# S5 stage: float32 products on two column tiles, and the order of the last gate

## The chip, the cores and the metric

One core of one Trainium2 chip runs the whole kernel. The metric is device time in microseconds, the median of the runs shown. An execution is also profiled: the profile gives its span, from the first instruction to the last, and each engine's work within it. The engines are PE (matrix products, with PEld for the loading of its stationary operand), DVE (vector), ACT (activations), POOL and SP (which only issues DMAs here).

## The reference, cut to what matters

Two layers on 256 tokens of width 1024, batch 1. Each layer adds half a SwiGLU block, a mixer, and half a SwiGLU block again to `h`. The mixer of the first layer is S5, a diagonal state-space layer, and the change lies in it; the second layer's mixer is attention.

```python
def s5_mixer(h, w_in, ..., w_glu, w_out):
    u = h @ w_in                                   # 64 groups of 16 channels
    ...                                            # lam, bb: discretised state matrices
    bu = einsum('bcgn,gpn->bcgp', u_c, bb)         # complex, 64 states a group
    st = associative_scan(lam * previous + bu)     # over the 256 positions
    y = einsum('bcgp,gnp->bcgn', st_re, c_re) - einsum('bcgp,gnp->bcgn', st_im, c_im)
    y = y + d_skip * u
    g = gelu(y)
    g = g * sigmoid(g @ w_glu)
    return g @ w_out
```

## The kernel before, in words

**Order of work.** The kernel is written as one program whose order on each engine is the order of the Python calls; nothing reorders it. Four positions are taken as one step of the scan, so 256 tokens are 64 steps, and every S5 product moves 64 columns. The 64 groups are worked in eight blocks `b` of four pairs of groups (`q`). The tables (`TA`, `TE`, `TB`) are made in the first SwiGLU stage, kept in DRAM and loaded by SP.

**Weights.** The large matrix products use two float32r parts of each float32 weight, a high part (`whi`) and a low part (`wlo`), and of each activation likewise. `Stream` brings the weights: SP loads a raw unit of 128 x 2048 into one of three buffers, and `split` cuts half a unit into `whi` (ACT, L84, or L90 where a gain is applied) and `wlo` (DVE, L85, or L91). `pump` does the next split in order if a slot is free, `get` fetches the two parts, `release` gives the slot back, and the second split of a unit frees the raw buffer for SP's next load. Where the calls of `pump` stand decides where the splits stand in the queues of ACT and DVE.

**The S5 stage.** In this order on PE, with the others beside it:

- `w_in(nh, t)`: four products of `h` with `w_in` into `psM`; ACT and DVE bring the result into `U`, 32 rows of channels a block.
- `t1(b)` (L982): eight float32 products, `TA` stationary (128 x 128) and `U` moving (64 columns), into an accumulator bank.
- `rot(b)`: DVE multiplies by `TE` (L1002 and L1003 from PSUM, L1004 and L1005 in SBUF) and scans (L1007, twice); POOL multiplies back in four instructions (L1011 to L1014) and leaves the states `hr`.
- `y_out(b)` (L1039 to L1041): for each of four `q` three float32 products, of `TB` with `U` and with the two parts of `hr`, into one `psR`; ACT applies the gelu (L1045, `yg`), DVE transposes (L1048, `gs`).
- `g_tr(b)`: two PE transposes (L1057) into a `psR`; ACT takes the high part (L1059, `xa`), DVE the low part (L1060), then ACT a float32 copy (L1061, `gf`). `psR` has two buffers in turn; at this place `y_out` has one of them and `g_tr` the other.
- `glu(b)` (L1074 to L1076): block `b` of `g @ w_glu`, 24 products of 256 columns, three for each of eight output chunks `o`, into four accumulator banks (two chunks a bank).
- `gate(i)`: for bank `i`, ACT's sigmoid (L1087), then DVE multiplies (L1089), makes the high part (L1091) and the low part (L1092).
- `so(b, t, n)`: the product with `w_out`, stationary from gate `b`'s output, 12 products of 512 columns for `b` of four and every `t` and half; the last two `b` run inside `boundary`, which adds the result to `h` (L369) and prepares the next stage's `x` by transposes (`prep`, L331, L333, L334).

From block 3 on one turn of the loop is

```python
for b in range(3, NB):
    y_out(b)
    glu(b - 3)
    if b + 3 < NB:
        t1rot(b + 3)
    g_tr(b - 1)
```

After it come `glu(5)`, `g_tr(7)`, a small activation that loads the sigmoid table (`warm`, L232), `glu(6)` and `glu(7)`, with `gate(i)` after each second chunk of `glu(7)`, then `so`. The dictionary `XO` gives, for each stage, the column at which the high and low parts of its `x` begin in their tile; `'g'` is that of the S5 gate.

Of the kernel before, what the change touches and what calls it, by code (L numbers as in the profile page):

```python
# [12 lines left out]
AF = mybir.ActivationFunctionType  # L13
# [12 lines left out]
TWO_PI = 2.0 * math.pi  # L26
MAGIC = 12582912.0

XO = {'f00': 124, 's5': 124, 'g': 0, 'f01': 80, 'f10': 8, 'moba': 124, 'f11': 8}
AO = (68, 68, 68, 68)  # L30
OO = 68

# [86 lines left out]
def trunk_kernel(ctx: ExitStack, tc, x, ffn_norm, ffn_w_gate, ffn_w_up, ffn_w_down, mix_norm,  # L119
# [17 lines left out]
    def psR():  # L137
        return pp.tile([128, 512], F32, name="pR", tag="R", bufs=2)
# [4 lines left out]
    mm = nc.tensor.matmul  # L143
# [85 lines left out]
    def warm(func):  # L229

        w = sp.tile([128, 1], F32, name="warm", tag="warm", bufs=1)
        nc.scalar.activation(w, ones[:, 0:1], func)  # L232
# [44 lines left out]
    st = Stream(nc, units, rp, hp)  # L277
# [37 lines left out]
    def home(pool, ph):  # L315

        xa = pool.tile([128, 4224], F32R, name="xa")
        v = xa[:, XO[ph]:XO[ph] + 4096].rearrange("p (i k c) -> p i k c", i=2, c=256)
        return v[:, 0], v[:, 1]

    def prep(t, n, ph, sq=True):

        if (ph, "x") not in X:
            X.clear()
            X[ph, "x"] = True
            X["h"], X["l"] = home(XP[0], ph)
        hh = h[t][:, n * 512:(n + 1) * 512]
        ps = psR()
        pv = ps.rearrange("p (k c) -> p k c", c=128)
        for k in range(4):  # L330
            nc.tensor.transpose(pv[:, k, :], hh[:, k * 128:(k + 1) * 128], ident)  # L331
        xh, xl = (X[p][:, n * 4:n * 4 + 4, t * 128:t * 128 + 128] for p in "hl")
        nc.scalar.activation(xh, pv, AF.Copy)  # L333
        nc.vector.tensor_tensor(xl, pv, xh.bitcast(F32), op=OP.subtract)  # L334
        if sq:
            squares(t, n)

    def squares(t, n):
        if n == 0:
            SS[t] = sp.tile([128, 2], F32, name="ss", tag="ss", bufs=4)  # L340
        hh = h[t][:, n * 512:(n + 1) * 512]
        sq = sp.tile([128, 512], mybir.dt.bfloat16, name="sq", tag="sq", bufs=1)
        nc.scalar.activation(sq, hh, AF.Square, accum_out=SS[t][:, n:n + 1])  # L343
        if n == 1:
            v = sp.tile([128, 1], F32, name="ms", tag="ms", bufs=4)
            nc.gpsimd.tensor_tensor(v, SS[t][:, 0:1], SS[t][:, 1:2], op=OP.add)  # L346
            nc.gpsimd.tensor_scalar(v, v, 1.0 / D, EPS, op0=OP.mult, op1=OP.add)
            r = sp.tile([128, 1], F32, name="rr", tag="rr", bufs=4)
            rsq(r, v, 1)
            Rr[t] = r  # L350
# [17 lines left out]
        hh = h[t][:, n * 512:(n + 1) * 512]  # L368
        nc.vector.scalar_tensor_tensor(hh, acc, scale, hh, op0=OP.mult, op1=OP.add)  # L369

    def boundary(nxt, parts, acc, scale, mid=None):

        if nxt is not None and nxt[0] == "f":
            order = [(0, 0), (1, 0), (0, 1), (1, 1)]
        else:
            order = [(0, 0), (0, 1), (1, 0), (1, 1)]
        for i in range(2):
            for part in parts[:-1]:
                part(*order[i])
            if mid is not None and i == 0:  # L380
                mid()
        for i, (t, n) in enumerate(order):
            for part in parts[-1:] if i < 2 else parts:
                part(t, n)
            finish(t, n, acc[2 * t + n], scale)
            if nxt is None:
                store(t, n)
            elif i:
                prep(*order[i - 1], nxt)

    def entry_hooks(ph):
        return {2: [lambda: prep(1, 1, ph)]}
# [562 lines left out]

    def s5(nxt, entry):
        V, P = nc.vector, nc.gpsimd
        wstack = ExitStack()
        wp = wstack.enter_context(tc.tile_pool(name="s5", bufs=1))
        S, H = {}, {}  # L960
        GT, GS = {}, {}
        acc = [None] * 4

        U = wp.tile([128, 32, 2, 32], F32, name="U")
# [11 lines left out]
        def t1(b):  # L976
            tv = TA.pop(b).rearrange("p (i q c) -> p i q c", i=2, c=128)
            ps = psA(b) if b < 4 else psM()
            for i in range(2):
                for q in range(4):  # L980
                    c = i * 256 + q * 64
                    mm(ps[:, c:c + 64], tv[:, i, q, :], U[:, 4 * b + q, :, :], start=True, stop=True)  # L982
            S[b] = ps

        def rot(b):
# [45 lines left out]
        def y_out(b):  # L1031
            tb = TB.pop(b)
            v2 = tb[:, 0:1024].rearrange("p (i q c) -> p i q c", i=2, c=128)
            v3 = tb[:, 1024:1536].rearrange("p (q c) -> p q c", c=128)
            ps = psR()
            hr = H.pop(b)
            for q in range(4):
                o = ps[:, q * 64:(q + 1) * 64]
                mm(o, v3[:, q, :], U[:, 4 * b + q, :, :], start=True, stop=False)  # L1039
                mm(o, v2[:, 0, q, :], hr[:, 0, q, :], start=False, stop=False)  # L1040
                mm(o, v2[:, 1, q, :], hr[:, 1, q, :], start=False, stop=True)  # L1041
            if b + 3 < NB:
                ld_b(b + 3)
            yg = wp.tile([128, 4, 2, 32], F32, name="yg", bufs=1)
            nc.scalar.activation(yg.rearrange("p q t c -> p (q t c)"), ps[:, 0:256], AF.Gelu_apprx_tanh)  # L1045
            gs = wp.tile([128, 2, 4, 32], F32, name="gs", bufs=2)
            for t in range(2):
                V.transpose(gs[:, t], yg[:, :, t, :])  # L1048
            GS[b] = gs

        def g_tr(b):
            ps = psR()
            gs = GS.pop(b)
            if b == 0:
                GT["h"], GT["l"] = home(xp, "g")
            for t in range(2):
                nc.tensor.transpose(ps[:, t * 128:(t + 1) * 128], gs[:, t].rearrange("p q c -> p (q c)"),  # L1057
                                    ident)
            nc.scalar.activation(GT["h"][:, b, :], ps[:, 0:256], AF.Copy)  # L1059
            V.tensor_tensor(GT["l"][:, b, :], ps[:, 0:256], GT["h"][:, b, :].bitcast(F32), op=OP.subtract)  # L1060
            nc.scalar.activation(gf[b // 2][:, b % 2, :], ps[:, 0:256], AF.Copy)  # L1061

        def glu(b, after=None):

            u = where["glu", b // 2]
            if b == 0:
                for i in range(4):
                    acc[i] = psA(i)
            gh, gl = GT["h"][:, b, :], GT["l"][:, b, :]
            wh, wl = st.get(u, b % 2)  # L1070
            for o in range(8):
                d = acc[o // 2][:, (o % 2) * 256:(o % 2) * 256 + 256]
                c = slice(o * 128, o * 128 + 128)
                mm(d, wh[:, c], gh, start=b == 0 and o % 2 == 0, stop=False, skip_group_check=True)  # L1074
                mm(d, wh[:, c], gl, start=False, stop=False, skip_group_check=True)
                mm(d, wl[:, c], gh, start=False, stop=b == NB - 1, skip_group_check=True)  # L1076
                if o == 7:
                    st.release(u, b % 2)
                if o == 3 and b < 7 or o == 7 and b in (3, 4, 5):
                    st.pump()  # L1080
                if after is not None and o % 2 == 1:
                    after(o // 2)

        def gate(i):

            sg = fp.tile([128, 2, 256], F32, name="sg", tag="gr", bufs=2)
            nc.scalar.activation(sg, acc[i].rearrange("p (a c) -> p a c", a=2), AF.Sigmoid)  # L1087
            g = gf[i]
            V.tensor_tensor(g, g, sg, op=OP.mult)  # L1089
            gh, gl = (GT[p][:, 2 * i:2 * i + 2, :] for p in "hl")  # L1090
            V.tensor_copy(gh, g)  # L1091
            V.tensor_tensor(gl, g, gh.bitcast(F32), op=OP.subtract)  # L1092

        def so(b, t, n, last=False):
            u = where["so", b]
            if b == 0:
                acc[2 * t + n] = psA(2 * t + n)
            gh, gl = (GT[p][:, 2 * b:2 * b + 2, :] for p in "hl")
            bank_mm(acc, t, n, gh, gl, u, [0, 1], b == 0, last)
# [20 lines left out]
        wstack.close()  # L1120
        lstack.close()
        XP[0] = xstack.enter_context(tc.tile_pool(name="xt2", bufs=1))
        glu(5)
        g_tr(7)
        warm(AF.Sigmoid)
        glu(6)
        glu(7, gate)
        for b in range(2):
            for t in range(2):
                for n in range(2):  # L1130
# [3 lines left out]
                        st.release(where["so", b], i)  # L1134
                st.pump(2 - b * t)

        boundary(nxt, [lambda t, n: so(2, t, n), lambda t, n: so(3, t, n, True)], acc, 1.0)
        for b in (2, 3):
            for i in range(2):
                st.release(where["so", b], i)  # L1140
# [204 lines left out]
    v2, rn, r2 = (sp.tile([128, 2], F32, name=n, tag=n, bufs=1) for n in ("ms2", "rn2", "rr2"))  # L1345
# [39 lines left out]
    for i, ph in enumerate(phases):  # L1385
        nxt = phases[i + 1] if i + 1 < len(phases) else None
# [59 lines left out]
```

## Time and profile before

| | |
|---|---|
| median of 3 runs | 1003.43 us (1003.33 to 1004.4) |
| the profiled execution's own time | 1005.22 us |
| its span | 1003.4 us |
| mean granted TensorE clock | 0.996 |
| busy: PE, PEld | 991.4 us, 887.4 us |
| busy: DVE, ACT, POOL | 702.9 us, 576.4 us, 166.5 us |

A timeline row reads: start and length in microseconds, engine, line, operation, tile written <- tiles read, for PE rows x columns of the stationary operand, the moving operand, the type, and how many instructions are merged; in brackets the idle time of the engine ahead of it and what ended it. A row of groups ends in busy time and mean nanoseconds of one instruction, then the idle time before. PE's records overlap, so the pitch of PE work is read from start to start. One float32 product is two records of PEld and PE in this trace; a float32r product is one. All times in the prediction are from the start of the span.

### The profile page before, as it was taken

Reading aid. Unit: us, or ns where it says so; the run is one execution under the profiler, and the core shown is the slowest. Engines: PE = TensorE matmul, PEld = TensorE weight load, DVE = VectorE, ACT = ScalarE, POOL = GpSimd, SP = SyncE. Lnnn points to the kernel's source line nnn. Section 1 sums busy time; section 2 is a strip of 40 time slices with the busy share of each in tenths; the row PEclk is TensorE's granted clock in tenths of the full one; section 3 lists DMA queues with packets and bytes.
Section 4 is the critical chain, followed back from the end, with each engine's and each line's share of the span. In section 5 each row is a group of like instructions: output and inputs, shape, how many; then the busy total and the mean of one; then the engine's idle time right before and its main releaser. Section 6 shows DMA issues by size and latency. Waiting matters only on the chain.

```text
span 1003.4 us, 16545 instructions
## 1 busy us (share of the span) xinstructions
PE 991.4 (99%) x6380; PEld 887.4 (88%) x6380; DVE 702.9 (70%) x1147; ACT 576.4 (57%) x1045; POOL 166.5 (17%) x330
## 2 busy tenths in 40 slices
PE   8999999999999999999999999999999999999998
PEld 7778888888998999999989999999888899999997
DVE  4799776857977677666657766665689667766662
ACT  6656778744245566555545655553798666555551
POOL 4881222113740100000010000000342010000000
PEclk8999999999999999999999999999999999999999
DMA  8877776886736466555536765655354456756531
GB/s 233 270 261 242 265 260 212 270 322 225 273 119 198 159 220 220 183 197 183 194 86 216 243 210 169 210 168 173 125 164 138 164 167 210 233 188 210 169 126 42
DMA packets 138079, 198.64 MB, mean 198 GB/s; under 512 B 16320, under 2 KB 109584, under 8 KB 137744
## 3 DMA queue, kind: packets, MB, share of 16 engines
q1 hardware_dynamic: 133808, 184.32, 56.8%
q0 software_dynamic: 3616, 12.66, 3.2%
q8 instruction: 50, 0.82, 0.4%
q10 hardware_dynamic: 576, 0.61, 0.3%
q14 instruction: 29, 0.24, 0.1%
HBM read 183.89 MB, written 13.66 MB: 197 GB/s over the span
## 4 chain that ended last, share of the span: by engine, by line
PE 84%; DVE 5%; POOL 5%; issue 3%; ACT 1%; DMA 1%; SPq 0%; POOLq 0%; ACTq 0%; DVEq 0%
PE pM L550 12%; PE pM L549 12%; PE pM L551 12%; PE pA L395 9%; PE pA L397 9%; PE pA L396 9%; PE pM L395 4%; PE pM L396 4%; PE pM L397 4%; DVE wlo L85 1%; POOL sc L684 1%; POOL qrs L304 1%; PE pR L331 1%; PE pA L469 1%; PE pR L878 1%
## 5 line engine op out<-in xcount | busy, mean ns | idle before, releaser
L549 PE MATMUL pM<-xa,whi 128*128 128x256 f32 x1056 | 295.7, 280 | 0.0
L550 PE MATMUL pM<-xa,whi 128*128 128x256 f32 x1056 | 294.9, 279 | 0.0
L551 PE MATMUL pM<-xa,wlo 128*128 128x256 f32 x1056 | 294.7, 279 | 0.0
L91 DVE SCALAR_TENSOR_TENSOR wlo<-raw,gT,whi 128x512 fp32r<-128x512 f32 x328 | 227.8, 748 | 69.3 <-ACT whi L90 69.2
L85 DVE TENSOR_TENSOR wlo<-raw,whi 128x1024 fp32r<-128x1024 f32 (+1 forms) x157 | 191.7, 1235 | 59.5 <-ACT whi L84 58.6
L90 ACT ACTIVATE whi<-raw,gT 128x512 fp32r<-128x512 f32 x328 | 213.4, 711 | 17.9 <-PE pA L397 14.0
L550 PEld LDWEIGHTS pM<-xa,whi 128*128 128x128 f32 x1056 | 198.5, 188 | 2.6
L549 PEld LDWEIGHTS pM<-xa,whi 128*128 128x128 f32 x1056 | 198.5, 188 | 2.3
L551 PEld LDWEIGHTS pM<-xa,wlo 128*128 128x128 f32 x1056 | 198.5, 188 | 0.0
L84 ACT ACTIVATE whi<-raw 128x1024 fp32r<-128x1024 f32 (+1 forms) x157 | 160.7, 1048 | 25.9 <-PE pA L397 6.8
L395 PE MATMUL pA<-whi,ah 128*128 128x512 f32 x352 | 138.8, 394 | 0.0
L396 PE MATMUL pA<-wlo,ah 128*128 128x512 f32 x352 | 137.6, 391 | 0.0
L397 PE MATMUL pA<-whi,al 128*128 128x512 f32 x352 | 137.6, 391 | 0.0
L564 ACT ACTIVATE sg<-gr 128x256 f32<-128x256 f32 x66 | 27.6, 418 | 164.6 <-DVE gr L561 164.6
L395 PE MATMUL pM<-whi,xa 128*128 128x512 f32 x288 | 119.3, 414 | 0.0
L396 PE MATMUL pM<-wlo,xa 128*128 128x512 f32 x288 | 113.0, 392 | 1.0 <-DVE wlo L85 0.8
L397 PE MATMUL pM<-whi,xa 128*128 128x512 f32 x288 | 112.6, 391 | 0.0
L346 POOL TENSOR_TENSOR ms<-ss 128x1 f32<-128x1 f32 x10 | 1.9, 193 | 474.5 <-ACT sq L343 474.5
L397 PEld LDWEIGHTS pA<-whi,al 128*128 128x128 f32 x352 | 66.1, 188 | 14.4
L395 PEld LDWEIGHTS pA<-whi,ah 128*128 128x128 f32 x352 | 66.1, 188 | 11.5
L396 PEld LDWEIGHTS pA<-wlo,ah 128*128 128x128 f32 x352 | 66.1, 188 | 11.3
L561 DVE TENSOR_TENSOR gr<-pM,rrow 128x512 f32<-128x512 f32 x66 | 45.4, 688 | 39.2 <-PE pM L551 39.1
(264 smaller groups left out, 1276.5 us busy)
## 6 DMA issues: line engine op xcount, KB each, us to landing
raw<-in_ffn_w_down_dram SPq DMA_DIRECT2D x44, 1024.0 KB, 5.2
raw<-in_ffn_w_gate_dram SPq DMA_DIRECT2D x80, 512.0 KB, 4.0
raw<-in_ffn_w_up_dram SPq DMA_DIRECT2D x80, 512.0 KB, 5.1
raw<-in_moba_w_qkv_dram SPq DMA_DIRECT2D x12, 1024.0 KB, 5.2
TB<-dB SPq DMA_DIRECT2D x8, 768.0 KB, 6.1
raw<-in_ffn_w_gate_dram SPq DMA_DIRECT2D x16, 256.0 KB, 4.4
raw<-in_ffn_w_up_dram SPq DMA_DIRECT2D x16, 256.0 KB, 4.6
dB<-tt POOLq DMA_DIRECT2D x16, 256.0 KB, 4.6
```

Source lines behind the costliest of these rows:

```text
L84: nc.scalar.activation(hi[:, c], r[:, c], AF.Copy)
L85: nc.vector.tensor_tensor(lo[:, c], r[:, c], hi[:, c].bitcast(F32), op=OP.subtract)
L90: nc.scalar.activation(hi[:, c], r[:, c], AF.Identity, scale=g)
L91: nc.vector.scalar_tensor_tensor(lo[:, c], r[:, c], g, hi[:, c].bitcast(F32), op0=OP.mult, op1=OP.subtract)
L395: mm(o, xh, wh, start=start, stop=False)
L396: mm(o, xh, wl, start=False, stop=False)
L397: mm(o, xl, wh, start=False, stop=stop)
L549: mm(o, a, xh, start=k == 0 and i == 0, stop=False, skip_group_check=True)
L550: mm(o, a, xl, start=False, stop=False, skip_group_check=True)
L551: mm(o, b, xh, start=False, stop=k == 7, skip_group_check=True)
L561: V.tensor_tensor(gr, ps.rearrange("p (i c) -> p i c", i=2), Rr["row"][:, None, :].to_broadcast([128, 2, 256]), op=OP.mult)
L564: nc.scalar.activation(sg, gr[:, 0, :], AF.Silu)
```

## The change

Each float32 product of `t1` and `y_out` (128 stationary columns, 64 moving ones) is written as two products of 64 stationary columns each, whose results go to partitions 0 to 63 and 64 to 127 of the same bank, that is, to two column tiles of the array. The last part is reordered: `g_tr(7)` stands right behind `g_tr(6)`, then two splits, the sigmoid table and `glu(5)`; `glu(6)` and `glu(7)` run for two chunks at a time, each pair followed by its gate. The calls of `pump` in `glu` are set anew: block 4 makes three splits, blocks 5 and 6 none. Two splits move from the following SwiGLU stage's first product into the boundary, behind its second and third parts. `XO['g']` goes from 0 to 8. The order on SP and on POOL is the same as before.

```diff
-XO = {'f00': 124, 's5': 124, 'g': 0, 'f01': 80, 'f10': 8, 'moba': 124, 'f11': 8}
+XO = {'f00': 124, 's5': 124, 'g': 8, 'f01': 80, 'f10': 8, 'moba': 124, 'f11': 8}
...
-    def boundary(nxt, parts, acc, scale, mid=None):
+    def boundary(nxt, parts, acc, scale, mid=None, pumps=()):
...
+            if i in pumps:
+                st.pump()
...
+        HALVES = (slice(0, 64), slice(64, 128))
...
-                    mm(ps[:, c:c + 64], tv[:, i, q, :], U[:, 4 * b + q, :, :], start=True, stop=True)
+                    for r in HALVES:
+                        mm(ps[r, c:c + 64], tv[:, i, q, r], U[:, 4 * b + q, :, :], start=True, stop=True)
...
-                o = ps[:, q * 64:(q + 1) * 64]
-                mm(o, v3[:, q, :], U[:, 4 * b + q, :, :], start=True, stop=False)
-                mm(o, v2[:, 0, q, :], hr[:, 0, q, :], start=False, stop=False)
-                mm(o, v2[:, 1, q, :], hr[:, 1, q, :], start=False, stop=True)
+                for i, (v, z) in enumerate(((v3[:, q], U[:, 4 * b + q]), (v2[:, 0, q], hr[:, 0, q]), (v2[:, 1, q], hr[:, 1, q]))):
+                    for r in HALVES:
+                        mm(ps[r, q * 64:(q + 1) * 64], v[:, r], z, start=i == 0, stop=i == 2)
...
-        def glu(b, after=None):
+        def glu(b, os=range(8)):
...
-            for o in range(8):
+            for o in os:
...
-                if o == 3 and b < 7 or o == 7 and b in (3, 4, 5):
+                if o == 3 and b < 5 or o == 7 and b in (3, 4) or o == 5 and b == 4:
                     st.pump()
-                if after is not None and o % 2 == 1:
-                    after(o // 2)
...
+        g_tr(7)
+        st.pump(2)
+        warm(AF.Sigmoid)
         glu(5)
-        g_tr(7)
-        warm(AF.Sigmoid)
-        glu(6)
-        glu(7, gate)
+        for i in range(4):
+            glu(6, (2 * i, 2 * i + 1))
+            glu(7, (2 * i, 2 * i + 1))
+            gate(i)
...
-        boundary(nxt, [lambda t, n: so(2, t, n), lambda t, n: so(3, t, n, True)], acc, 1.0)
+        boundary(nxt, [lambda t, n: so(2, t, n), lambda t, n: so(3, t, n, True)], acc, 1.0, pumps=(1, 2))
```

## The prediction

> **What bounds the kernel now.** I read the page first: its span, the busy times, and the groups that concern this change.
>
> ```profile
> span 1003.4 us, 16545 instructions
> PE 991.4 (99%) x6380; PEld 887.4 (88%) x6380; DVE 702.9 (70%) x1147; ACT 576.4 (57%) x1045; POOL 166.5 (17%) x330
> ```
>
> Over the whole span PE is the bound. That is an average over stages, so I read the S5 stage by stretches (columns: stretch, its length, busy time of PE, PEld, DVE, ACT, POOL, granted clock, DMA share, GB/s).
>
> ```profile
> 250.00:262.00 12.00, 12.00 (x95) 11.40 (x94) 11.93 (x21) 2.66 (x4) 9.29 (x9) 1.00 0.69 241
> 262.00:274.00 12.00, 11.86 (x106) 11.64 (x105) 11.40 (x26) 4.39 (x11) 8.94 (x9) 1.00 0.84 312
> ```
>
> Here PE and DVE are both full: DVE has 0.07 us left in the first 12. So a faster PE meets DVE at once. DVE and POOL work out the rotation and scan (`rot`) of each of the eight blocks, and `y_out` waits for them. The timeline of POOL shows the rhythm: its first instruction for blocks 0, 1 and 7 (first, second and last of eight L1011 rows).
>
> ```profile
> 244.31 1.29 POOL L1011 TENSOR_TENSOR pv<-zo,TE 128x512 f32<-128x512 f32 x1 [12.35 <-DMA TA<-dA]
> 249.86 2.13 POOL L1011 TENSOR_TENSOR pv<-zo,TE 128x512 f32<-128x512 f32 x1 [1.28 <-issue]
> 286.93 1.29 POOL L1011 TENSOR_TENSOR pv<-zo,TE 128x512 f32<-128x512 f32 x1 [2.08 <-issue]
> ```
>
> The first cycle, with nothing else in it, takes 5.55 us; the seven take 42.6, since splits lie in some. None of that work is changed by the diff. Only its start depends on PE, by the first `t1`, in the timelines of PE and DVE:
>
> ```profile
> 238.96 1.89 PE L982 MATMUL pA<-U,TA 128*128 128x64 f32 x16
> 240.66 0.47 PE L395 MATMUL pM<-whi,xa 128*128 128x512 f32 x1
> ...
> 238.83 1.23 DVE L85 TENSOR_TENSOR wlo<-raw,whi 128x1024 fp32r<-128x1024 f32 x1 [0.24 <-ACT whi L84]
> 240.89 0.69 DVE L1002 TENSOR_TENSOR wv<-pA,TE 128x512 f32<-128x512 f32 x1 [0.80 <-PE pA L982]
> ```
>
> **One float32 product, before and after.** The sixteen records of L982 are eight products, two records (a load of 128 stationary columns, then a pass of 64 moving ones) each. From 238.96 to 240.66 that is 1.70 us, 0.106 a record, 0.21 a product. A row with smaller stationaries says which half of the record costs: L878 passes the same 64 columns over 32 stationary ones.
>
> ```profile
> 97.09 0.39 PE L396 MATMUL pM<-wlo,xa 128*128 128x512 f32 x1
> 97.32 0.40 PE L397 MATMUL pM<-whi,xa 128*128 128x512 f32 x1
> 97.64 1.08 PE L878 MATMUL pR<-zc,mp 128*32 128x64 f32 x16
> 98.65 0.29 PE L880 MATMUL pR<-dg,cst 32*32 32x64 f32 x2
> ...
> L878 PEld LDWEIGHTS pR<-zc,mp x128: 106/110/110, 97.6 to 199.2; 128*32 128x32 f32 x128
> ```
>
> Sixteen records take 98.65 - 97.64 = 1.01 us, and about 0.1 of that is the change to the next form, so 0.057 a record. The pass costs no more than 0.057; the 128-column load makes it 0.106.
>
> After the change a product is four records of 64 stationary columns, two in each column tile. I estimate a record in one tile at 0.057, since a load of half of 128 columns is half of 0.106. If the second tile works beside the first, the product costs two records, 0.115 us; if the tiles take turns, four, 0.23. No row of before has two column tiles in a row, so these are the two ends. I take 0.115: on L878 sixteen loads of 0.110 each lie inside a microsecond that also holds sixteen passes, so loads already run beside passes where nothing forbids it. The Trainium skill (TensorEngine Tiling (Array Packing), Key Properties) says that different tiles can load weights and multiply in parallel; by it the product would also be 0.115.
>
> Then `t1` (8 products) goes from 1.70 to 0.92 and `y_out` (12) from 2.60 to 1.38. Over eight of each PE would be freed of (0.78 + 1.22) x 8 = 16 us. Going into another array form costs: L878 starts 0.32 after the last wide pass (97.64 less 97.32), where a wide one starts 0.23 after another (97.32 less 97.09), so 0.09. The diff makes 13 groups of tiled products, 26 changes, 2.3 us.
>
> **What of this reaches the end.** The first `t1` is done 0.78 earlier, less 0.09: `rot(0)` starts 0.7 earlier (DVE is free from 240.06, the end of its L85). From there DVE runs in the same order with the same work, so each rotation is 0.7 earlier and no more. PE, freed of 16 us, waits. The place that decides is `y_out(6)`: its psR buffer is that of `y_out(5)`, which ACT reads (L1045) only after its copy L1061, which follows DVE's L1060, which stands behind the last rotation.
>
> ```profile
> 286.71 0.40 DVE L1060 TENSOR_TENSOR xa<-pR,xa 128x256 fp32r<-128x256 f32 x1
> ...
> 287.14 0.39 ACT L1061 ACTIVATE gf<-pR 128x256 f32<-128x256 f32 x1 [4.16 <-DVE xa L1060]
> 287.43 0.38 ACT L1045 ACTIVATE yg<-pR 128x256 f32<-128x256 f32 x1
> ...
> 288.18 0.33 PE L1039 MATMUL pR<-U,TB 128*128 128x64 f32 x2
> 290.78 0.36 PE L1074 MATMUL pA<-xa,whi 128*128 128x256 f32 x1
> 293.95 0.33 PE L1039 MATMUL pR<-U,TB 128*128 128x64 f32 x2
> 296.54 0.36 PE L1074 MATMUL pA<-xa,whi 128*128 128x256 f32 x1
> 299.50 0.38 PE L1057 MATMUL pR<-cst,gs 128*128 128x128 f32 x2
> ```
>
> ACT releases it at 287.81, and `y_out(6)` began at 288.18: PE was only 0.37 late. After: release at 287.1, so `y_out(6)` gains 1.1. From there PE is the chain again: two `y_out` at 1.38 + 0.18 for two changes of form in place of 2.60 each save 2.1. `glu(4)` starts at 296.5 - 3.2 = 293.3. Of 16 us, 3.2 come through. New waits on PE lie ahead of `g_tr(3)`, `g_tr(4)` and near `g_tr(0)`; queued behind them is only PE's own work.
>
> **The tail.** ACT and DVE set the end of the stage, by gate 0.
>
> ```profile
> 295.28 0.38 ACT L1061 ACTIVATE gf<-pR 128x256 f32<-128x256 f32 x1 [0.75 <-DVE xa L1060]
> 296.83 0.38 ACT L1045 ACTIVATE yg<-pR 128x256 f32<-128x256 f32 x1 [1.17 <-PE pR L1041]
> 297.11 2.00 ACT L84 ACTIVATE whi<-raw 128x1024 fp32r<-128x1024 f32 x2
> 305.41 1.28 ACT L232 ACT_TABLE_LOAD   x1
> 307.76 1.06 ACT L1087 ACTIVATE sg<-pA 128x512 f32<-128x512 f32 x2
> ...
> 298.20 2.36 DVE L85 TENSOR_TENSOR wlo<-raw,whi 128x1024 fp32r<-128x1024 f32 x2 [0.44 <-ACT whi L84]
> 309.03 0.69 DVE L1089 TENSOR_TENSOR gf<-gf,sg 128x512 f32<-128x512 f32 x1
> 309.75 0.43 DVE L1091 CAST xa<-gf 128x512 fp32r<-128x512 f32 x1
> 310.32 0.47 PE L395 MATMUL pA<-whi,xa 128*128 128x512 f32 x1 [1.62 <-DVE xa L1091]
> ```
>
> Now PE waits 1.62 us for gate 0 before the first `so`. After, `glu(6)` and `glu(7)` run bank by bank, so gate 0's inputs are there 36 products before PE needs its output, some 4.4 us by `glu(4)`'s 24 in 2.96. But the splits were moved ahead of it: three in `glu(4)`, two behind `g_tr(7)`, all before the sigmoids in ACT's queue. Step by step: `gf(5)` ends 0.7 earlier, at 294.96; `yg(7)` follows to 295.3 (1.9 earlier than now) and `gs(7)` on DVE to 295.8. Three splits: ACT to 298.3, DVE (1.18 each, the first behind ACT's first at 296.3) to 299.9. `xa(6)`, `gf(6)`, `xa(7)`, its DVE half, `gf(7)`, each about 0.37: to 301.8. Two more splits on ACT, 2.0: 303.8. Table load and its small activation, 1.5: 305.3. Sigmoid 0.6, L1089 0.69, L1091 0.46: 307.05, where it was 310.18. PE meanwhile: `glu(4)` from 293.3, `g_tr(6)`, `g_tr(7)`, `glu(5)` to 299.4, a wait of 0.8 for `xa(6)` and `xa(7)`, 48 products: 306.0. So PE still waits 1.1 for gate 0, and `so` starts at 307.1 instead of 310.3: **3.2 us earlier**, as much as `glu(4)` gained. Gates 1 to 3 follow at the old distance (L1089, L1091, L1092 are unchanged), and everything behind is PE's.
>
> The other edits. `XO['g']` from 0 to 8 moves the operand of `glu`: the groups of the page and of the stage show what an address may do, 3 ns a product on 192.
>
> ```profile
> L550 PE MATMUL pM<-xa,whi 128*128 128x256 f32 x1056 | 294.9, 279 | 0.0
> ...
> L1075 PE MATMUL pA<-xa,whi 128*128 128x256 f32 x64 | 18.1, 282 | 0.0
> ```
>
> At most 0.6 us either way; on the path lie `glu(3)` and `glu(4)`, 48 products, 0.1, taken with the rest as nothing. Two splits of f01's weights move from f01's first product into the boundary. Each is two L90 on ACT and two L91 on DVE, and L91 takes 0.75:
>
> ```profile
> L91 DVE SCALAR_TENSOR_TENSOR wlo<-raw,gT,whi 128x512 fp32r<-128x512 f32 x328 | 227.8, 748 | 69.3 <-ACT whi L90 69.2
> ```
>
> They lie beside the last `so` products; without that cover 1.5 each, 3.0 in all. I take 0 and keep +1 for the range. The order on SP and POOL is unchanged; the raw buffers freed by the moved splits reload earlier, with DMA at 0.65 to 0.85 of its time here.
>
> **The sum.** -3.2 on a span of 1003.4. The profiled execution took 1005.22 us, 1.8 outside its span; the runs have a median of 1003.43, at which I place the span. Forecast 1003.4 - 3.2 = **1000.2**; own range 998.0 to 1001.6 (chain offsets of 1 us on either side, boundary +1, XO -0.6).
>
> **Rivals.**
> *The clock falls.* PE now gets waits of up to 4 us in the stage (near 258 to 262 and 277 to 280). At the start of the kernel the clock did fall behind a thin stretch:
>
> ```profile
> 4.00:8.00 4.00, 2.25 (x14) 1.64 (x13) 1.29 (x4) 1.73 (x4) 3.92 (x9) 1.00 0.90 287
> 8.00:12.00 4.00, 3.97 (x14) 2.68 (x13) 2.37 (x4) 2.20 (x6) 0.00 (x0) 0.54 1.06 364
> 12.00:16.00 4.00, 4.00 (x15) 3.21 (x14) 1.45 (x6) 2.36 (x8) 0.00 (x0) 0.61 1.09 348
> ```
>
> Eight microseconds at 0.54 and 0.61 lose 3.4 us of work. Against it: the 1.62 us wait before `so` is followed by a full clock,
>
> ```profile
> 310.00:315.00 5.00, 4.68 (x20) 3.65 (x21) 4.83 (x9) 4.00 (x6) 0.00 (x0) 1.00 0.72 211
> ```
>
> and a fall near 262 or 280 is covered by the next wait for DVE. Only a fall that lasts through `y_out(6)` to `y_out(7)` counts, 3.4 at most: 1000 to 1003.5, middle 1002. The Trainium skill (TensorE: Matmul & The Clock Gate, The HAM clock gate) has half rate after an idle window of about 3.4 us; by it the wait near 260 would be long enough.
>
> *The tiles take turns.* A product costs 0.23, PE stays the bound: 160 products x 0.01 more = 1.6, changes of form 2.3, less 1.6 to 2.0 for the gate: +2.1, **1005.5**. The load row is for it: if there is one path for stationary columns, 128 of them cost the same in halves.
>
> *Loads and passes exclude each other between the tiles* (slower). Then each of the four records costs its load and its pass one after the other, up to a whole record of now, 0.106: 0.42 a product, +0.21 x 160 = 34 us, plus 2: up to **1038**. It decides as soon as a product costs over 0.22. Against it stands the L878 row. The Trainium skill (TensorE: Matmul & The Clock Gate, Part 3, The mechanism) says that a load overlaps passes in flight only in other row groups; the tiles here share all row groups, so by that rule this rival holds, but on L878 loads overlap passes in the same rows.
>
> **How the numbers follow.** Forecast 0.62, clock 0.10, turns 0.16, exclusion 0.12. About 0.2% (2.0 us) is what a measurement of this kernel can tell from no change. The forecast lies 1.2 beyond that: of its 0.62, 0.56 is faster and 0.06 the same. Clock: 0.04 faster, 0.04 same, 0.02 slower. Turns, at the edge: 0.08 same, 0.08 slower. Exclusion: 0.12 slower. So faster 0.60, same 0.18, slower 0.22. The range runs from 998.0 to 1005.5, the middle of turns; it leaves out exclusion (0.12) and half of turns (0.08).
>
> **What would show it.** Right: blocks of L986 about 0.95 us, `y_out` about 1.4; PE idle some 3 us before `g_tr(3)` and 2 before `g_tr(4)`, POOL's eight starts still 42.6 us from first to last, 0.7 earlier; first `so` near 307 with PE waiting about 1 us for the gate. Wrong: tiled blocks as long as before or longer (turns, exclusion), a granted clock under 0.9 between 262 and 296, a rotation cycle under 5.5 us, or a stall in f01's first product or the boundary.

## The result, and the profile after

| | before | after |
|---|---|---|
| median of 8 runs each | 1003.68 us (1003.17 to 1004.4) | 1000.77 us (1000.07 to 1002.21) |
| span of the profiled execution | 1003.4 us | 999.3 us |
| mean granted TensorE clock | 0.996 | 0.996 |
| from the first `t1` to f01's first product | 94.77 us | 91.80 us |

The ratio is 0.9967, with a 95% interval from 0.9958 to 0.9976: faster by 3.3 us (2.4 to 4.2); the medians differ by 2.9.

The spans differ by 4.1 us, more than that. 1.2 of it lies ahead of the change: the first `t1` begins at 237.74 instead of 238.96. Part of it is the clock at the start of the kernel, where nothing that the diff touches runs. The prediction shows it at 0.61 between 12 and 16 us of the execution of before; the same stretch of after:

```profile
12.00:16.00 4.00, 4.00 (x22) 3.30 (x21) 2.50 (x8) 3.88 (x11) 0.00 (x0) 1.00 1.09 349
```

So the two traces are compared from the first `t1` on. In the timelines of PE, the first product of f01, the SwiGLU stage that follows (L549 before, L551 after), stands at 333.73 and 329.54, which is 94.77 and 91.80 behind the first `t1`: 2.97 us come from the stage. What follows takes the same time in both (669.7 and 669.8 us to the end of the span).

First the page of after: PE is busy 11.5 us less and holds 320 records more (160 products, two more records each).

```profile
span 999.3 us, 17186 instructions
PE 979.9 (98%) x6700; PEld 870.9 (87%) x6700; DVE 703.3 (70%) x1147; ACT 575.7 (58%) x1045; POOL 167.2 (17%) x330
```

The stage by stretches (columns as in the prediction): PE, full or nearly so in both stretches before, has 4.1 us free in the first. DVE is as full as it was.

```profile
250.00:262.00 12.00, 7.86 (x163) 6.74 (x163) 11.40 (x23) 3.82 (x8) 9.28 (x10) 0.94 0.85 306
262.00:274.00 12.00, 12.00 (x230) 11.07 (x227) 11.93 (x23) 3.58 (x9) 8.94 (x9) 0.92 0.78 270
```

The first `t1` in PE's timeline, from its start to the next group's: 1.08 us, where it was 1.70. It holds 32 records now.

```profile
237.74 1.15 PE L986 MATMUL pA<-U,TA 128*64 128x64 f32 x32
238.82 0.50 PE L397 MATMUL pM<-whi,xa 128*128 128x512 f32 x1
```

POOL's timeline, first, second and last of the eight rotations: 42.70 us from first to last, and 4.62 us behind the first `t1` instead of 5.35.

```profile
242.36 1.29 POOL L1015 TENSOR_TENSOR pv<-zo,TE 128x512 f32<-128x512 f32 x1 [11.74 <-DMA TA<-dA]
247.93 2.14 POOL L1015 TENSOR_TENSOR pv<-zo,TE 128x512 f32<-128x512 f32 x1 [1.28 <-issue]
285.06 1.27 POOL L1015 TENSOR_TENSOR pv<-zo,TE 128x512 f32<-128x512 f32 x1 [2.04 <-issue]
```

The waits of PE in the stage (columns: who waited for whom, us in total, times, the longest). The first row is `g_tr(3)` and `g_tr(4)`, 2.08 and 1.94; the second is `g_tr(0)`; the third is the first `so`. The first two have no counterpart before.

```profile
PE pR L1060 <- ACT gf L1064: 4.0, 2, 2.1
PE pR L1060 <- DVE gs L1051: 4.0, 1, 4.0
PE pA L397 <- DVE xa L1092: 0.5, 1, 0.5
```

The place that the prediction calls deciding, in the timelines of ACT and PE. ACT's copy (L1064) waits 4.77 us for DVE; `yg(5)` follows to 285.94; `y_out(6)` begins at 286.08 and `glu(4)` at 292.40. What held PE last is one step ahead of the place that the prediction names: `g_tr(4)` needs the `psR` that the same copy frees at 285.66, starts at 285.72, and `y_out(6)` follows it 0.36 later.

```profile
285.28 0.38 ACT L1064 ACTIVATE gf<-pR 128x256 f32<-128x256 f32 x1 [4.77 <-DVE xa L1063]
285.56 0.38 ACT L1048 ACTIVATE yg<-pR 128x256 f32<-128x256 f32 x1
...
285.72 0.44 PE L1060 MATMUL pR<-cst,gs 128*128 128x128 f32 x2 [1.94 <-ACT gf L1064]
286.08 0.34 PE L1044 MATMUL pR<-U,TB 128*64 128x64 f32 x4
...
287.63 0.38 PE L1077 MATMUL pA<-xa,whi 128*128 128x256 f32 x1
...
290.85 0.34 PE L1044 MATMUL pR<-U,TB 128*64 128x64 f32 x4
...
292.40 0.38 PE L1077 MATMUL pA<-xa,whi 128*128 128x256 f32 x1
```

The tail, timelines of ACT, DVE and PE: the splits, the table, gate 0 and the first `so`.

```profile
293.94 2.96 ACT L84 ACTIVATE whi<-raw 128x1024 fp32r<-128x1024 f32 x3
296.79 0.39 ACT L1062 ACTIVATE xa<-pR 128x256 fp32r<-128x256 f32 x1
...
300.34 2.00 ACT L84 ACTIVATE whi<-raw 128x1024 fp32r<-128x1024 f32 x2
302.35 1.28 ACT L232 ACT_TABLE_LOAD   x1
...
303.76 1.07 ACT L1088 ACTIVATE sg<-pA 128x512 f32<-128x512 f32 x2
...
304.37 0.69 DVE L1090 TENSOR_TENSOR gf<-gf,sg 128x512 f32<-128x512 f32 x1 [0.58 <-ACT sg L1088]
305.09 0.43 DVE L1092 CAST xa<-gf 128x512 fp32r<-128x512 f32 x1
...
305.66 0.48 PE L397 MATMUL pA<-whi,xa 128*128 128x512 f32 x1 [0.53 <-DVE xa L1092]
```

Counted from each trace's first `t1`, the gain builds up like this:

| start of | before | after | gain |
|---|---|---|---|
| POOL's first rotation | 5.35 | 4.62 | 0.73 |
| `y_out(6)` | 49.22 | 48.34 | 0.88 |
| `glu(4)` | 57.58 | 54.66 | 2.92 |
| first `so` | 71.36 | 67.92 | 3.44 |
| f01's first product | 94.77 | 91.80 | 2.97 |

### The profile page after: what moved, and what is told of

The parts are those of the page before. It is cut to its first block, busy times and chain, and to the rows that moved or that the text cites. A ratio compares the mean times of both kernels' runs of the same rounds, so it can differ in the third digit from the quotient of the medians.

```text
span 999.3 us, 17186 instructions
## 1 busy us (share of the span) xinstructions
PE 979.9 (98%) x6700; PEld 870.9 (87%) x6700; DVE 703.3 (70%) x1147; ACT 575.7 (58%) x1045; POOL 167.2 (17%) x330
## 4 chain that ended last, share of the span: by engine, by line
PE 86%; DVE 7%; POOL 3%; issue 2%; ACT 2%; DMA 1%; SPq 0%; ACTq 0%; DVEq 0%
PE pM L552 12%; PE pM L551 12%; PE pM L553 12%; PE pA L397 9%; PE pA L399 9%; PE pA L398 9%; PE pM L397 5%; PE pM L398 5%; PE pM L399 5%; DVE wlo L85 2%; DVE zo L1011 1%; POOL sc L686 1%; PE pR L331 1%; PE pR L880 1%; ACT whi L84 1%
## 5 line engine op out<-in xcount | busy, mean ns | idle before, releaser
L551 PE MATMUL pM<-xa,whi 128*128 128x256 f32 x1056 | 295.7, 280 | 0.0
L551 PEld LDWEIGHTS pM<-xa,whi 128*128 128x128 f32 x1056 | 198.5, 188 | 2.3
L397 PEld LDWEIGHTS pA<-whi,ah 128*128 128x128 f32 x352 | 66.1, 188 | 11.5
L563 DVE TENSOR_TENSOR gr<-pM,rrow 128x512 f32<-128x512 f32 x66 | 45.5, 689 | 40.6 <-PE pM L553 40.5
```

Of the source, the lines that this page charges most:

```text
L397: mm(o, xh, wh, start=start, stop=False)
L551: mm(o, a, xh, start=k == 0 and i == 0, stop=False, skip_group_check=True)
L563: V.tensor_tensor(gr, ps.rearrange("p (i c) -> p i c", i=2), Rr["row"][:, None, :].to_broadcast([128, 2, 256]), op=OP.mult)
```

## The experiments

The theory after the result was this: the chain of DVE and POOL paces the stage up to `y_out(6)`, so most of what PE saves turns into waits; the change gains only where it starts that chain earlier and where PE is alone behind it, and in the tail. The rivals were that PE's amount of work is still what counts, and that DVE's amount of work alone is the bound. Each ratio below is against runs of the kernel before on the same chip; two chips were used.

### The two halves of the change

Column tiles alone, the order of before kept:

```diff
-  mm(ps[:, c:c + 64], tv[:, i, q, :], U[...])
+  for r in HALVES:
+      mm(ps[r, c:c + 64], tv[:, i, q, r], U[...])
   ... the same in y_out
```

> The kernel before with the column tiles alone (t1 and y_out); last gate, splits and XO as before. My theory (the rotation chain on DVE and POOL lets 3 us through, then the tail): glu(4) 3 us earlier as in the changed kernel, but gate 0 behind glu(7) as before, so first so some 2 us earlier than before, 1001.5 to 1002.2 against 1003.7. Rival, the gain comes from the order of the last gate alone: 1003.7, no change. Rival, tiles' 16 us of PE time come through: below 995.

Measured: 1002.6 us (1001.47 to 1004.87), ratio 0.9989 (0.998 to 0.9998).

The order of the tail alone, with `XO` and the pumps, and whole products:

```diff
-  HALVES = (slice(0, 64), slice(64, 128))
+  HALVES = (slice(0, 128),)
```

> The changed kernel with whole products (128 stationary columns) in t1 and y_out; gate order, splits and XO as changed. My theory: y_out(7) stays where it was before, the tail gains up to 1.3 us by the gate's order and loses 0.4 in so by XO: 1002.3 to 1003.4. Rival, the order alone makes the gain: 1000.8.

Measured: 1002.43 us (1001.73 to 1003.88), ratio 0.9986 (0.9977 to 0.9995).

Each half gains something over 1 us, neither as much as both. Their ratios multiply to 0.9975; the whole change has 0.9967 and the intervals overlap, so no more than a sum is needed. The traces say the same: counted from the first `t1`, the first `so` comes 1.94 us earlier with the tiles alone (69.42) and 1.77 with the tail alone (69.59), where both together gain 3.44. With whole products PE still waits 0.38 us for gate 0. The tiles alone came out 0.4 us short of what was expected. The profiled execution of that kernel, 1004.87 us and the slowest of its eleven, shows one way to lose time: PE waits 2.27 us for gate 0 and the clock falls behind that wait, where nothing covers it.

```profile
308.68 0.59 PE L395 MATMUL pA<-whi,xa 128*128 128x512 f32 x1 [2.27 <-DVE xa L1092]
```

The stretches behind it, the granted clock in the third column from the end:

```profile
308.00:312.00 4.00, 3.32 (x8) 2.50 (x9) 3.83 (x8) 2.64 (x4) 0.00 (x0) 0.61 0.76 227
312.00:316.00 4.00, 4.00 (x18) 3.31 (x17) 3.83 (x7) 4.00 (x6) 0.00 (x0) 0.96 0.11 38
```

The first 72 products of `so` then take 18.02 us instead of before's 16.64, at the same operand offset. This execution has a mean granted clock of 0.991, the other ten 0.994 to 0.996, so it isn't shown that such a fall makes the median's 0.4; that stays open.

### Do the tiles work side by side?

All products of one tile in a row, then all of the other:

```diff
-  for i in range(2):
-      for q in range(4):
-          for r in HALVES:
+  for r in HALVES:
+      for i in range(2):
+          for q in range(4):
   ... the same in y_out
```

> The changed kernel with the loop over the two column tiles outermost, so that all of a block's products of one tile follow each other: the same 64-column loads and passes, but no neighbour in the other tile. If the gain on PE needs the two tiles side by side: a product costs four records of 0.057, 0.23 us, t1 blocks about 1.85 us and y_out 2.8; PE is the bound again and the time is 1005 to 1008. If the shorter loads alone make it: as the changed kernel, 1000.8.

Measured: 1004.3 us (1003.42 to 1005.79), ratio 1.0002 (0.9993 to 1.0011); the whole gain is gone, tail included. PE's timeline:

```profile
237.63 1.90 PE L986 MATMUL pA<-U,TA 128*64 128x64 f32 x32
239.46 0.50 PE L397 MATMUL pM<-whi,xa 128*128 128x512 f32 x1
```

The same 32 records take 1.83 us instead of 1.08, a record of one tile 0.052, and PE waits nowhere before the tail. Less 0.18 for two changes of form, a product of two tiles takes 0.206 us here, where `y_out` of the changed kernel has three products in 0.35 us (286.48 to 286.83), 0.117 each. So the tiles do work side by side here, but only when neighbouring instructions go to different ones. The blocks came as expected (1.83 for 1.85, `y_out` 2.76 for 2.8), the time did not (1005 to 1008): the expectation left out that the tail keeps its gain. From the first `t1` to f01 the trace has 95.38 us, 0.61 over before, where the tail alone had 93.47, 1.30 under it.

### The offset of the gate's operand

```diff
-XO = {..., 'g': 8, ...}
+XO = {..., 'g': 0, ...}     # in the other kernel: 124
```

> The changed kernel with XO['g'] back at 0. In its trace the so products stand 0.231 to 0.235 us apart where before had 0.227, and glu's 0.120 as before. If the offset makes that: so back at 0.227, 0.4 us less, 1000.3. If the order of splits beside so makes it: no change, 1000.8.

> The changed kernel with XO's entry g at 124 instead of 8, the value that stage s5 has. Theory (the offset of the operand in SBUF sets 7 ns of each following product): the 72 products of the next stage's first blocks take 16.6 us as with 0, not 17.06, and the time falls by 0.4 us to 1000.3. Rival (124 costs the gate products what 8 saves them): 1000.8 us or up to 0.5 us more.

Measured: 1000.84 us (999.8 to 1002.64), ratio 0.9966 (0.9953 to 0.9979) with 0, and 1000.59 us (1000.0 to 1000.81), ratio 0.9966 (0.9953 to 0.9978) with 124. The times don't tell them from the change; the traces do. The groups of PE between 312 and 321 us, in the middle of `so`, with 8 (count, busy us, mean ns of one):

```profile
L398 PE MATMUL pA<-wlo,xa 128*128 128x512 f32 x14 | 5.5, 396 | 0.0
```

and with 124:

```profile
L398 PE MATMUL pA<-wlo,xa 128*128 128x512 f32 x14 | 5.4, 389 | 0.0
```

With 8 the record of a product is 7 ns longer, and the first 72 products of `so` (of 96) take 17.06 us; with 124 they take 16.63, with 0 16.64. The tail alone, with 8 too, has 17.06. From the first `t1` to f01's first product the trace with 124 has 91.28 us, 0.52 less than the change. A `glu` block takes 2.91 and 2.93 us with 8 (blocks 3 and 4), 2.93 and 2.93 with 124, 2.98 with 0 (block 4). In the trace with 0 the clock fell to 0.75 and 0.82 between 286 and 294 us, behind a wait of 1.91 us, and `so` began 0.48 later than with 8, which cancels the gain there. That is one execution, the slowest of its six (1002.64 us), of which 1.5 us lie ahead of the first `t1`; why the median didn't fall isn't shown.

### Is PE's time free where it waits?

Products of ones by ones that nobody reads, in the waits of PE:

```diff
+  fill(psA(0), 14)      # ahead of g_tr(0); 7 each ahead of g_tr(3) and g_tr(4)
   g_tr(0)
```

> The changed kernel with idle products added: 14 float32 products of ones (128x128) ahead of the first gate transpose, 7 ahead of the fourth and 7 ahead of the fifth, which is where PE now waits 3.98, 2.07 and 1.94 us. They compute nothing that is read. Theory (VectorE's and GpSimd's rotation chain sets the pace in this stretch, PE's waits are spare time): the added 6 us of PE work cost nothing; 1000 to 1000.8 us, and at most 1 us less where the waits had let the clock fall. Rival (PE's amount of work is still the bound, the waits are only where it is seen): near 1006 us.

Measured: 1000.88 us (1000.65 to 1002.51), ratio 0.9973 (0.9963 to 0.9983): no loss that shows, for 28 products more. PE's waits at these three places shrink from 8.0 to 2.5 us, and from the first `t1` to f01's first product it is 91.80 us, to the hundredth that of the change. In the changed kernel the clock had fallen behind the wait of 3.98 us (ends at 260.01):

```profile
258.00:262.00 4.00, 1.83 (x26) 1.58 (x28) 3.47 (x11) 1.17 (x4) 2.72 (x3) 0.82 0.95 329
262.00:266.00 4.00, 4.00 (x98) 3.58 (x96) 3.96 (x9) 0.98 (x3) 2.30 (x4) 0.75 1.03 394
```

With the fill it stays whole in the same stretches:

```profile
258.00:262.00 4.00, 3.17 (x60) 2.67 (x60) 3.47 (x11) 1.38 (x4) 2.72 (x3) 1.00 1.00 367
262.00:266.00 4.00, 3.87 (x89) 3.49 (x90) 3.97 (x11) 0.74 (x3) 2.31 (x4) 1.00 1.02 408
```

A clock restored, and nothing gained: the fall had been paid out of the next wait. PE's amount of work isn't the bound up to `y_out(6)`.

### What makes the rotation as long as it is

One addition more at the end of each rotation on POOL, which stood idle for 1.28 us there:

```diff
   P.tensor_tensor(hr[:, 1], pv[0][:, 1], pv[1][:, 0], op=OP.subtract)
+  P.tensor_tensor(pv[0][:, 0], pv[0][:, 0], pv[1][:, 1], op=OP.add)
```

> The changed kernel with one more addition of 128x256 in SBUF on GpSimd at the end of each rotation, behind the state's difference. Nothing reads its result, and GpSimd stood idle for 1.28 us there. Theory (GpSimd's and VectorE's work on SBUF exclude each other, so that GpSimd's idle time is not free while VectorE scans): every rotation grows by 0.6 to 0.9 us, GpSimd's eight starts spread over 46.9 to 49 us instead of 42.7, the fifth gate block and what follows come 3 to 5 us later, and the time is 1003.5 to 1005.5 us. Rival (the engines work side by side and the idle time is free): 42.7 us and 1000.8 us as before.

Measured: 1004.27 us (1003.75 to 1005.01), ratio 1.0002 (0.9993 to 1.001), 3.5 us over the change. POOL's timeline, first and last rotation: 46.30 us, a little under what was expected.

```profile
242.69 1.29 POOL L1015 TENSOR_TENSOR pv<-zo,TE 128x512 f32<-128x512 f32 x1 [11.73 <-DMA TA<-dA]
...
288.99 1.28 POOL L1015 TENSOR_TENSOR pv<-zo,TE 128x512 f32<-128x512 f32 x1 [1.95 <-issue]
```

The idle time wasn't free. The opposite, POOL's two last steps moved to DVE for blocks 0 to 5:

```diff
+  # in rot(b), behind the two wv products
+  if late:
+      late.pop(0)()
...
-  P.tensor_tensor(hr[:, 0], ...); P.tensor_tensor(hr[:, 1], ...)
+  if b < 6: late.append(lambda: states(V))
+  else:     states(P)
```

> The changed kernel with the two last steps of a rotation (the state's sum and difference) moved from GpSimd to VectorE in blocks 0 to 5, behind the next block's first products. Theory (the chain in which GpSimd and VectorE take turns paces the stretch, 42.7 us from the first to the last of GpSimd's eight starts): with 1.2 us less of GpSimd's work a block and 0.6 us more of VectorE's, that falls to 39.5 to 40.5 us, PE's waits shrink, and the time falls by 2 to 3 us, to 998 to 999 us. Rival (VectorE's amount of work is the bound, busy 11.93 of 12 us in part of it): no gain or a loss, 1000.8 to 1004 us.

Measured: 999.34 us (999.08 to 999.79), ratio 0.9955 (0.9942 to 0.9967), 1.4 us under the change by medians and 1.2 by the ratios and the traces (90.59 us from the first `t1` to f01, for 91.80), though DVE does more; 998 to 999 was expected. From first to last rotation:

```profile
242.03 1.30 POOL L1017 TENSOR_TENSOR pv<-zo,TE 128x512 f32<-128x512 f32 x1 [11.74 <-DMA TA<-dA]
...
283.09 1.28 POOL L1017 TENSOR_TENSOR pv<-zo,TE 128x512 f32<-128x512 f32 x1 [2.05 <-issue]
```

41.06 us: 1.6 less than 42.70, but not the 39.5 to 40.5 that was expected. The groups of DVE between 240 and 292 us tell why it worked and why by less. The scan and the first sum `zi` (L1008) of the changed kernel:

```profile
L1011 DVE TENSOR_TENSOR_SCAN zo<-rh,zi 128x260 f32<-128x260 f32 x16 | 12.4, 812 | 0.0
L1008 DVE TENSOR_TENSOR zi<-wv,wv 128x256 f32<-128x256 f32 x8 | 7.0, 875 | 0.3
```

The scan with the extra addition on POOL:

```profile
L1011 DVE TENSOR_TENSOR_SCAN zo<-rh,zi 128x260 f32<-128x260 f32 x16 | 15.4, 1000 | 0.0
```

Scan, sum and the moved step, where POOL has only its two products left:

```profile
L1013 DVE TENSOR_TENSOR_SCAN zo<-rh,zi 128x260 f32<-128x260 f32 x16 | 10.3, 684 | 0.0
L1010 DVE TENSOR_TENSOR zi<-wv,wv 128x256 f32<-128x256 f32 x8 | 3.4, 420 | 0.1
L1020 DVE TENSOR_TENSOR hr<-pv,pv 128x256 f32<-128x256 f32 x6 | 2.5, 425 | 3.6 <-POOL pv L1018 3.6
```

One cycle of the changed kernel, in the timelines of POOL and DVE, in order of time:

```profile
254.36 1.29 POOL L1015 TENSOR_TENSOR pv<-zo,TE 128x512 f32<-128x512 f32 x1 [1.28 <-issue]
254.78 0.67 DVE L1006 TENSOR_TENSOR wv<-pA,TE 128x512 f32<-128x512 f32 x1
255.60 1.28 POOL L1016 TENSOR_TENSOR pv<-zo,TE 128x512 f32<-128x512 f32 x1
256.09 1.07 DVE L1008 TENSOR_TENSOR zi<-wv,wv 128x256 f32<-128x256 f32 x1
256.96 0.78 POOL L1017 TENSOR_TENSOR hr<-pv,pv 128x256 f32<-128x256 f32 x1
257.08 0.94 DVE L1009 TENSOR_TENSOR zi<-wv,wv 128x256 f32<-128x256 f32 x1
257.70 0.90 POOL L1018 TENSOR_TENSOR hr<-pv,pv 128x256 f32<-128x256 f32 x1
257.95 1.80 DVE L1011 TENSOR_TENSOR_SCAN zo<-rh,zi 128x260 f32<-128x260 f32 x2
```

With `hr` moved, POOL is idle from 256.10 to 258.90 while DVE does the six:

```profile
256.14 0.43 DVE L1020 TENSOR_TENSOR hr<-pv,pv 128x256 f32<-128x256 f32 x1 [0.87 <-POOL pv L1018]
257.48 1.28 DVE L1013 TENSOR_TENSOR_SCAN zo<-rh,zi 128x260 f32<-128x260 f32 x2
```

A sum takes 420 ns with POOL idle. Beside POOL the first takes 875: in the cycle above it starts at 256.09 and ends at 257.16, shortly after POOL's second product has ended at 256.88. A scan takes 684 with POOL idle, 812 with the two short instructions of `hr` beside it, 1000 with the third. The first products (`wv`), which read PSUM and one operand in SBUF, take 0.67 to 0.68 us in all of them, POOL at work or not. So DVE's instructions with both inputs in SBUF take turns with POOL's, and what counts is the sum of both engines' turns. Moving `hr` makes two turns shorter, but they stay in the same line: one undisturbed cycle is POOL's two products (2.5) and then six instructions of DVE on SBUF (2.8), 5.33 us (253.57 to 258.90) where it was 5.52 (254.36 to 259.88). The Trainium skill (SBUF — State Buffer, Who interferes with whom) states it as a rule: a VectorE instruction with two SBUF inputs contends with a GpSimd instruction that reads SBUF, and the order of issue decides which of them is held up. The rows above agree, `wv`'s 0.67 too.

### Put together

> The state's sum and difference on VectorE in blocks 0 to 5, idle products (10, 7 and 7) in PE's waits, and the weight-load offset of this stage's operand (XO, entry g) back at 0. If GpSimd's and VectorE's chain is the bound and PE's waits let the clock fall: 997.5 to 998.5 us. If the shorter chain leaves PE's waits shorter than the added products: 999 to 1001 us.

> The state's sum and difference on VectorE in blocks 0 to 5, and XO's entry g at 124; no idle products. If the two gains add (1.4 and 0.2 to 0.4 us): 998.9 to 999.1 us. If the shorter chain had made the offset's loss invisible: 999.3 us.

> As the kernel before it, with idle products (10, 7 and 7) in PE's waits. If a fallen clock costs time once the chain is shorter: 998.2 to 998.5 us, 0.4 us less than without them. If PE's waits cover it still: the same as without them, 998.9 to 999.1 us.

| kernel (all with `hr` on DVE) | median | ratio |
|---|---|---|
| fill, `XO` g at 0 | 998.62 us (998.23 to 999.41) | 0.9948 (0.9934 to 0.9961) |
| no fill, g at 124 | 998.84 us (998.17 to 999.36) | 0.9944 (0.993 to 0.9959) |
| fill, g at 124 | 998.3 us (998.06 to 1000.29) | 0.9941 (0.9927 to 0.9955) |

All three are under both kernels, some 2 us under the changed one. Whether the fill adds anything is open: at 124, with it and without it, the traces have 89.71 and 89.65 us from the first `t1` to f01's first product, and the intervals overlap. Without it, the three executions with a mean clock of 0.998 took 998.17 to 998.57 us and the three with 0.994 or 0.995 took 999.12 to 999.36; with it, five of six had 1.0 and took 998.06 to 998.6. Where in the kernel the clock fell isn't shown by that: the sixth, 1000.29, began its first `t1` 1.9 us later than the trace without the fill. The first kernel came out 0.1 us above the 997.5 to 998.5 that was expected, the second just under its 998.9 to 999.1, the third inside the 998.2 to 998.5 for a fill that adds. What the traces account for is the shorter rotation and the offset.

## Why the prediction was right

The forecast was 1000.2 us, 3.2 less; it came to 1000.77, 2.9 less by medians and 3.3 by the ratio. The stage's path was right; that the sum lies so near is in part luck, since two misses of opposite sign are in it, 0.2 too little up to `so` and 0.47 too much behind it. Its steps:

- **One float32 product.** 0.115 us was taken, of the ends 0.115 and 0.23. It is 0.117 in a run of products; `t1` takes 1.08 us and `y_out` 1.55 with the changes of form, by the prediction 0.92 + 0.18 and 1.38 + 0.18. The 0.09 for a change of form held. The choice between the two ends was right, but the row that it rests on, L878, couldn't make it: all its products write the same 32 partitions, one column tile, and a record of 0.052 in one tile also stands where the tiles don't overlap (0.206 a product, with all of one tile in a row). That 0.115 came out hangs on the order of the instructions, which the prediction doesn't weigh.
- **Only 3.2 of 16 us come through.** Held, with the waits in their places: 3.98 ahead of `g_tr(0)`, 2.08 and 1.94 ahead of `g_tr(3)` and `g_tr(4)` (about 3 and 2 were said for the latter two). Eight `t1` and eight `y_out`, at 1.08 and 1.55 for 1.70 and 2.60, free 13.4 us of PE, the changes of form counted in. POOL's eight starts take 42.70 us, 0.73 earlier (42.6 and 0.7). The prediction had this from DVE being full, and that reason was wrong in part: DVE's time in that count holds turns spent waiting for POOL, and with more work on DVE the stage got shorter. What paces it is both engines' SBUF work in one line.
- **`y_out(6)` and `glu(4)`.** 1.1 and 3.2 were said, 0.88 and 2.92 came. The 0.2 is `g_tr(4)`: the prediction starts `y_out(6)` as soon as `yg(5)` frees its `psR`, but `g_tr(4)`, held by the same copy of ACT, stands ahead of it. The two `y_out` saved 2.0 (2.1 said).
- **The tail.** The chain of ACT and DVE was followed step by step: 307.05 for the end of L1092 and a wait of 1.1. Shifted by the 1.22 us that the two traces differ by, it ended at 306.74, and PE waited 0.53, because the gate came 0.3 sooner and PE, whose `glu(4)` began 0.3 later, arrived later. `so` gained 3.44 (3.2 said).
- **The mis-sized term.** `XO` g from 0 to 8 was taken as nothing within 0.6 either way, and on `glu` alone. The same entry places the operand that the gate writes for `so`. There it costs 0.42 us in the first 72 products (17.06 against 16.64), all on the path. From the first `so` to f01 it is 23.88 us against 23.41, which takes the gain from 3.44 to 2.97. It stayed inside the bound that the range had.
- **The splits in the boundary** cost nothing that shows: with the splits moved and `XO` g back at 0, the stretch from the first `so` to f01 takes 23.41 us, as before. The 0.47 is all the offset's.
- **The rivals.** *Exclusion of loads and passes* (the rule on row groups that the prediction cites) fell: a product takes 0.117 us, not up to 0.42, in tiles that share all rows. *Turns* is what the kernel with all of one tile in a row shows, at 0.206 instead of 0.23. *The clock* did fall, to 0.75 between 262 and 266 us. The prediction names a clock under 0.9 there as a sign of being wrong, but also says that a fall near 262 would be covered, and the fill shows that it was. In the traces of the tiles alone and of `XO` g at 0 it fell later, and time was lost: 1.38 us within `so` in the one, 0.48 ahead of it in the other.

## What to carry to other kernels

When a change speeds up the engine that is busy most, follow the chain of the next engine through the stage first: here some 13 us off PE and a new order of the tail were worth 3, about 1 of it from the tiles alone, and moving two small instructions between the other two engines was worth a third to a half as much again. Idle time of POOL beside a busy DVE isn't spare time, and a busy DVE isn't proof of DVE work: compare the mean of one instruction with and without the neighbour. Alternate column tiles from one instruction to the next; at this size (64 moving columns) they gain nothing otherwise.

## What the runs showed that was not expected

- The same 32 records of PE take 1.08 or 1.83 us by their order alone.
- A DVE instruction of 420 ns takes 875 beside POOL, and one short instruction a rotation in POOL's idle time cost 3.5 us.
- The clock fell behind waits of about 2 us in some traces and not in others: 0.61 behind 2.27 us, 0.75 behind 1.91; in the changed kernel's trace it stayed at 1.00 behind 2.08 and 1.94. The page that the prediction cites (the Trainium skill, TensorE: Matmul & The Clock Gate, The HAM clock gate) puts the idle window at about 3.4 us; these rows show falls behind shorter ones.
- The column at which the stationary operand begins in its SBUF tile is worth 7 ns in the record of a product of 512 columns (389 with 0 or 124, 396 with 8).
